# Layer 0 of a hybrid encoder projects x without its norm, and starts while x and weights land

## The chip, the core and the metric

The kernel runs on one core of a Trainium2 chip. Its engines are PE (matrix products), ACT (functions and copies, line by line), DVE and POOL (elementwise work), and SP, which only issues DMAs here. Each has its own queue and takes its instructions in order; they wait for one another by semaphores. PE reads operands from SBUF and writes sums to PSUM, from where ACT and DVE fetch them. The metric is device time in microseconds, the median over runs.

## The reference, cut to what matters

Two layers (`DEPTH = 2`) over 256 positions of width 2048:

```python
h = x
for i in range(DEPTH):
    hn = _rmsnorm(h, norm_g[i])                       # h * rsqrt(mean(h*h) + eps) * gain
    u = hn @ w_in[i]
    a_val, a_glu, a_z, q, k, v, b_z = jnp.split(u, offs, axis=-1)
    ya = _conformer_conv(a_val, a_glu, ...)           # GLU, depthwise conv of width 31, LayerNorm, SiLU
    ya = ya * jax.nn.silu(a_z)
    yb = _window_attention(q, k, v, bias_band, sink[i]) * jax.nn.silu(b_z)
    h = h + jnp.concatenate([ya, yb], axis=-1) @ w_out[i]
    e = _rmsnorm(p[i] @ w_pe[i], pe_g[i])             # embedding
    h = h + e * jax.nn.sigmoid(h @ w_pg[i])
return _rmsnorm(h, final_g)
```

The norm's root is one number per position. It can therefore be applied to x ahead of the projection, or to the projection's results, per position.

## The kernel before

All matrices stand transposed: 128 channels on the partitions, 256 positions along the free axis. A product of 128 x 128 weights with 128 x 256 of the input is made three times, since weights and input are each split into a high part in a shortened format and a low part, the rest (`mm3`, L398: high x high, high x low, low x high; L401 to L403).

Weights come as halves: 1024 columns of 128 partitions, 512 KB. Two make a chunk of 1 MB, loaded by SP into one of three raw buffers (`load`). `split` casts a half on ACT (L168) to its high part and subtracts it on DVE (L171) for the low part, into one of five buffers. The program asks for splits some four halves ahead (`ahead`, `get`); a half feeds 24 products on PE. Halves are numbered in the order of use in a layer: 0 to 3 embedding (`w_pe`), 4 to 11 the first two tiles of the convolution group's value and gate columns, 12 to 35 its other six tiles, 36 to 39 k, 40 to 43 v, then b_z and q by turns, then a_z, w_out, w_pg.

The order on PE, ACT and DVE is that of the program text (`manual_schedule`). After each half `pump` runs: it moves side generators on by one step (embedding's squares, the bias table, attention) and then takes some steps of the convolutions, 3.3 per half in this part of the layer. A step is a tap, one instruction on DVE (L566), but for the first of a tile, which is ACT's.

The start of layer 0: PE warms up with products of zeros; x, p and chunks of weights are loaded over the queues of SP and ACT. Embedding's products p @ w_pe run first, unsplit, straight from the raw weights (L487), while ACT squares x and DVE sums the squares (L392). From the sum come the root of the norm as a column (`rstd_col`: products with ones, a power on POOL, L361) and as a row over positions (`rstd_row`). `operand` then multiplies x by gain and row on DVE (L455) and splits it (L458, L459) into `hg`, the projection's input. A tile's result goes from PSUM through `glu`: ACT's sigmoid (L575), DVE's multiply (L576). k is split by ACT and DVE into `keys` (L599, L601); the gates zb pass Silu on ACT (L688); q is scaled and split into `qq` (L695 on ACT, L696 on DVE), which the scores `sc` (L636) need on PE. Embedding's squares are summed on POOL (L392), beside the convolution tiles; the bias table (`bias_prep`) has one product on PE (L329) and a copy on DVE (L331).

Of the kernel before, what the change touches and what calls it, by code (L numbers as in the profile page):

```python
# [10 lines left out]
F32 = mybir.dt.float32  # L11
# [45 lines left out]
NWARM = 6  # L57
QQ = ((4, 5), (2, 4))
# [21 lines left out]
def weight_halves():  # L80
# [39 lines left out]
HALVES = weight_halves()  # L120
NHALF = len(HALVES)
# [8 lines left out]
def trunk_kernel(ctx: ExitStack, tc: tile.TileContext, xT, pT, wst, par, gain, relb, sinkp, onehot, out):  # L130
# [23 lines left out]
    state = {"raw": -1, "spl": 3, "credit": 0.0}  # L154
# [8 lines left out]
    def split(h):  # L163
        raw = raws[h // 2][:, h % 2, :]
        w = wspl.tile([P, 2 * HALF + 64], F32R, tag="w", name=f"w{h}")
        w = w[:, SHIFT:SHIFT + 2 * HALF].rearrange("p (t n) -> p t n", t=2)
        hi, lo = w[:, 0], w[:, 1]
        nc.scalar.copy(hi, raw)  # L168
        spl[h] = w
        if h not in (4, 5):  # L170
            nc.vector.tensor_sub(lo, raw, hi.bitcast(F32))  # L171

    def first_lo(h):

        w = spl[h]
        nc.vector.tensor_sub(w[:, 1], raws[h // 2][:, h % 2, :], w[:, 0].bitcast(F32))

    def ahead(h):

        while state["spl"] < min(h, TOT - 1):  # L180
# [4 lines left out]
            if HALVES[n % NHALF][0] != "w_pe" or n >= NHALF:  # L185
                split(n)
            state["spl"] = n

    def get(h):

        r = h % NHALF
        if r < 12:
            ahead(h + (r | 1) + 2 - r)
        else:
            ahead(h + LS)
        return spl.pop(h)
# [66 lines left out]
    def load_p(l):  # L263
        pf = wk.tile([P, 2, S], F32, name=f"p{l}", tag="v", bufs=1)
        (nc.sync if l == 0 else nc.gpsimd).dma_start(pf, pT[l])
        return pf

    def load_half(c, x, eng=nc.sync, n=1):

        if c not in raws:  # L270
            raws[c] = wraw.tile([P, 2, HALF], F32, tag="raw", name=f"raw{c}")
        w = HALF // n
        for i in range(n):
            eng.dma_start(raws[c][:, x, i * w:(i + 1) * w], wst[c, :, x * HALF + i * w:x * HALF + (i + 1) * w])

    def load_x(k, eng=nc.sync):
        eng.dma_start(h[k // 8][:, k % 8:k % 8 + 4, :], xT[:, k:k + 4, :])

    h = halves(bigt("x"))

    load_half(0, 0, nc.scalar, 2)
    pf = load_p(0)
    load_half(0, 1)
    load_x(0, nc.scalar)
    load_x(4)
    load_half(1, 0, nc.scalar)
    load_x(8)
    load_x(12)
    load_half(1, 1)
    load_half(2, 0)  # L290
    gains = cst.tile([P, (DEPTH + 1) * KT], F32, name="gains")
    nc.sync.dma_start(gains, gain)
    load_half(2, 1)
    state["raw"] = 2
    pars = cst.tile([P, DEPTH * PW], F32, name="pars")
    nc.sync.dma_start(pars, par)
# [16 lines left out]
    nc.sync.dma_start(relt[0:NUM_BUCKETS, :], relb)  # L313
    oh = wk.tile([NUM_BUCKETS + 1, NREL], F32, name="oh", tag="sq", bufs=3)
    nc.sync.dma_start(oh, onehot)
    sinkt = cst.tile([P, DEPTH * NQ], F32, name="sinkt")
    nc.sync.dma_start(sinkt, sinkp.partition_broadcast(P))
# [94 lines left out]
    def steps(os, X, starts, stop):  # L412

        parts = []
        for _ in os:
            name, _, k0, nk = HALVES[Cursor.h % NHALF]
# [22 lines left out]
    for l in range(DEPTH):  # L439

        e = halves(bigt(f"e{l}"))
        eacc = wk.tile([P, 2, S], F32, name="eacc", tag="hacc")
# [26 lines left out]
        def copied(j, b, e=e):  # L469
            nc.scalar.copy(e[j // 8][:, j % 8:j % 8 + 2, :], b)  # L470

        for q in range(4):
            n = Cursor.h
            Cursor.h += 1
            if l:
                w = get(n).rearrange("p t (j k c) -> p t j k c", j=4, k=2)
            else:
                raw = raws[n // 2][:, n % 2, :].rearrange("p (j k c) -> p j k c", j=4, k=2)
            for jj in range(0, 4, 2):
                j = 4 * q + jj  # L480
                b = bank("e")
                for x in range(2):
                    for k in range(2):
                        if l:
                            mm3(b[:, x, :], w[:, :, jj + x, k, :], pp[:, :, k, :], x == 0 and k == 0, k == 1)
                        else:
                            nc.tensor.matmul(b[:, x, :], raw[:, jj + x, k, :], pf[:, k, :], start=x == 0 and k == 0,  # L487
                                             stop=k == 1, skip_group_check=True)
                if l == 0 and j // 2 < 4:
                    for k in (4 * (j // 2), 4 * (j // 2) + 2):  # L490
                        if k < KT - 2:
                            square_acc(hacc, h[k // 8][:, k % 8:k % 8 + 2, :], k == 0, nc.vector)
                    if j // 2 == 3:
                        sq = wk.tile([P, 2, S], F32, name="sq", tag="sq", bufs=3)
                        nc.scalar.activation(sq, h[1][:, 6:8, :], AF.Square)
                        hparts = halves_of(sq) + [fold(hacc)]
                if j // 2 == QQ[l][0]:
                    dg = rstd_col(hparts, D, f"rh{l}")
                    ahead(5 if l == 0 else Cursor.h - 1 - q + 5)
                if j // 2 == QQ[l][1]:  # L500
# [439 lines left out]
```

## Time and profile before

| | |
|---|---|
| median of 3 runs | 936.67 us (936.56 to 936.84) |
| the profiled execution's own time | 938.7 us |
| its span, first to last instruction | 936.9 us |
| mean granted clock of PE | 0.996 |
| PE busy | 923.9 us, 99% |
| DVE busy | 767.6 us, 82% |
| ACT busy | 549.2 us, 59% |
| POOL busy | 82.0 us, 9% |
| HBM read | 177.09 MB |

How to read it: the busy time of PE is modelled, and a PE that is busy is not PE at its peak. Rows of a timeline give start, duration, engine, line, operation, tiles and, in brackets, how long the engine stood idle before it and for whom. Rows of windows give, for each engine, busy time and number of instructions, then the granted clock, the share of busy DMA engines and GB/s. The chain is followed back from the last instruction, at each step to what released it.

### The profile page before, as it was taken

The page shows a single profiled execution, that of the slowest core. Times are in us where ns is not written, and L with a number is a line of the kernel's source. Part 1 is how long each engine was busy: PE and PEld are TensorE (multiplying, and loading weights), DVE is VectorE, ACT ScalarE, POOL GpSimd, SP SyncE. Part 2 cuts the span into 40 slices and gives each one's busy share as a digit, 9 for nine tenths or more (in the row PEclk, how much of TensorE's full clock was granted, in tenths as well). Part 3 has the DMA queues.
Part 4 walks back from the last instruction along what each step waited for, and adds up shares of the span by engine and source line. Part 5 has one row for each costly group of instructions (what it writes and reads, how often), then busy time and mean ns, then how long its engine had stood idle before and what let it go on. Part 6 is the DMA issues. An engine that isn't in the chain of part 4 may idle for free.

```text
span 936.9 us, 19106 instructions
## 1 busy us (share of the span) xinstructions
PE 923.9 (99%) x7960; PEld 909.7 (97%) x7960; DVE 767.6 (82%) x1282; ACT 549.2 (59%) x830; POOL 82.0 (9%) x79
## 2 busy tenths in 40 slices
PE   8999999999999999999999999999999999999995
PEld 7999999999999999999999999999999999999995
DVE  3999999998887786787679999999888877777663
ACT  4655454878874555554566445568788546445551
POOL 0013001001000000011102100100100000000111
PEclk9999999999999999999999999999999999999999
DMA  7674656555547455546555556565555554654532
GB/s 298 226 250 150 220 180 230 190 196 175 189 171 247 166 209 212 191 181 230 211 189 193 181 212 226 174 213 196 183 169 180 193 197 152 247 183 179 200 114 91
DMA packets 29011, 182.55 MB, mean 195 GB/s; under 512 B 3595, under 2 KB 4156, under 8 KB 9084
## 3 DMA queue, kind: packets, MB, share of 16 engines
q1 hardware_dynamic: 24284, 165.70, 50.1%
q0 software_dynamic: 3344, 12.88, 4.2%
q10 hardware_dynamic: 1296, 2.75, 0.8%
q8 instruction: 62, 1.02, 0.4%
q14 instruction: 25, 0.20, 0.1%
HBM read 177.09 MB, written 4.23 MB: 194 GB/s over the span
## 4 chain that ended last, share of the span: by engine, by line
PE 75%; DVE 19%; ACT 2%; issue 2%; DMA 1%; ACTq 0%; DVEq 0%
DVE cz L566 8%; DVE w L171 8%; PE o L401 6%; PE o L402 6%; PE o L403 6%; PE g L401 6%; PE g L403 6%; PE g L402 6%; PE ag L403 4%; PE ag L401 4%; PE ag L402 4%; PE za L401 3%; PE za L403 3%; PE za L402 3%; PE av L679 2%
## 5 line engine op out<-in xcount | busy, mean ns | idle before, releaser
L171 DVE TENSOR_TENSOR w<-raw,w 128x1024 fp32r<-128x1024 f32 x306 | 375.1, 1234 | 99.5 <-ACT w L168 98.6
L168 ACT CAST w<-raw 128x1024 fp32r<-128x1024 f32 x308 | 315.6, 1046 | 157.8 <-PE ag L403 42.5
L566 DVE SCALAR_TENSOR_TENSOR cz<-az,pars,cz 128x241 f32<-128x241 f32 (+11 forms) x480 | 215.9, 499 | 1.0
L401 PE MATMUL ag<-hg,w 128*128 128x256 f32 x512 | 141.8, 277 | 0.0
L403 PE MATMUL ag<-hg,w 128*128 128x256 f32 x512 | 141.6, 277 | 0.0
L402 PE MATMUL ag<-hg,w 128*128 128x256 f32 x512 | 141.5, 276 | 0.0
L403 PE MATMUL g<-h,w 128*128 128x256 f32 x512 | 141.3, 276 | 0.0
L401 PE MATMUL g<-h,w 128*128 128x256 f32 x512 | 141.3, 276 | 0.0
L402 PE MATMUL g<-h,w 128*128 128x256 f32 x512 | 141.3, 276 | 0.0
L401 PEld LDWEIGHTS ag<-hg,w 128*128 128x128 f32 x512 | 96.1, 188 | 0.9 <-ACT u L575 0.8
L403 PEld LDWEIGHTS ag<-hg,w 128*128 128x128 f32 x512 | 96.2, 188 | 0.1
L402 PEld LDWEIGHTS ag<-hg,w 128*128 128x128 f32 x512 | 96.1, 188 | 0.0
L401 PEld LDWEIGHTS g<-h,w 128*128 128x128 f32 x512 | 96.1, 188 | 0.0
L402 PEld LDWEIGHTS g<-h,w 128*128 128x128 f32 x512 | 96.1, 188 | 0.0
L403 PEld LDWEIGHTS g<-h,w 128*128 128x128 f32 x512 | 96.1, 188 | 0.0
L401 PE MATMUL za<-hg,w 128*128 128x256 f32 x256 | 71.7, 280 | 0.0
L401 PE MATMUL o<-yb,w 128*128 128x256 f32 x256 | 71.6, 280 | 0.0
L401 PE MATMUL q<-hg,w 128*128 128x256 f32 x256 | 71.5, 279 | 0.0
L401 PE MATMUL zb<-hg,w 128*128 128x256 f32 x256 | 71.5, 279 | 0.0
L402 PE MATMUL o<-yb,w 128*128 128x256 f32 x256 | 71.0, 277 | 0.0
L402 PE MATMUL q<-hg,w 128*128 128x256 f32 x256 | 71.0, 277 | 0.0
L403 PE MATMUL zb<-hg,w 128*128 128x256 f32 x256 | 71.0, 277 | 0.0
(223 smaller groups left out, 2264.4 us busy)
## 6 DMA issues: line engine op xcount, KB each, us to landing
raw<-in_wst SPq DMA_DIRECT2D x153, 1024.0 KB, 4.9
bias<-fscr POOLq DMA_DIRECT2D x16, 384.0 KB, 3.9
raw<-in_wst SPq DMA_DIRECT2D x4, 512.0 KB, 7.9
az<-in_xT POOLq DMA_DIRECT2D x4, 512.0 KB, 6.0
hscr<-e POOLq DMA_DIRECT2D x2, 1024.0 KB, 5.6
az<-hscr POOLq DMA_DIRECT2D x4, 512.0 KB, 5.4
x<-in_xT SPq DMA_DIRECT2D x3, 512.0 KB, 8.2
out_t<-og ACTq DMA_DIRECT2D x4, 256.0 KB, 3.0
```

What stands on the lines that cost most here:

```text
L168: nc.scalar.copy(hi, raw)
L171: nc.vector.tensor_sub(lo, raw, hi.bitcast(F32))
L401: nc.tensor.matmul(o, w[:, 0], x[:, 0], start=start, stop=False, skip_group_check=True)
L402: nc.tensor.matmul(o, w[:, 0], x[:, 1], start=False, stop=False, skip_group_check=True)
L403: nc.tensor.matmul(o, w[:, 1], x[:, 0], start=False, stop=stop, skip_group_check=True)
L566: nc.vector.scalar_tensor_tensor(acc[:, t, lo_:hi_], a[:, t, lo_ + s:hi_ + s], w(k), acc[:, t, lo_:hi_], ALU.mult, ALU.add)
L679: nc.tensor.matmul(o[hh * HD:(hh + 1) * HD, x, :], v[:, kt, g * HD:(g + 1) * HD], pt[hh][:, kt, :], start=x == 0 and kt == 0, stop=kt == 1 ...
```

## The change

In layer 0 the projection's input is x times gain, without the root. So it does not wait for the sum of squares: x and the weights of the first two tiles are loaded in pieces, in the order of use, and PE runs their products in four blocks of four k-tiles. ACT makes the high part of x times gain and DVE the low part (one instruction each per k-tile); weights are split by half a half (`split_part`). The sums of squares are made by POOL, and the root's column is asked for in the fourth block.

Every result of layer 0's projection is then multiplied by the root: in `evicted`, a DVE instruction that reads PSUM and writes a tile in SBUF (value and gate columns, k, b_z, q, a_z), and for v by the scale of ACT's copy. Sigmoid, Silu, the splits of k and the scaling of q read that tile.

Embedding's products of layer 0 come behind the first two tiles, split like all others (96 products instead of 64 plain ones), and the evictions of the two tiles stand between them. p, parameters and tables are loaded later, from `small_loads`; each of four tiles gets a memset on DVE ahead of it. `embed` (the bias table and embedding's squares) begins behind embedding's products. One warm-up product is added, the root of embedding's norm is asked for five steps later, and layer 1 keeps its order.

```diff
-NWARM = 6
+NWARM = 7
...
-    for q in range(4):
-        out.append(("w_pe", q, 0, 2))
+    if l:
+        out += W_PE
     for ts in FIRST_TILES:
...
+        if l == 0 and len(ts) == 2:
+            out += W_PE
...
+    def split_part(h, c):
+        if h not in spl:
+            w = wspl.tile([P, 2 * HALF + 64], F32R, tag="w", name=f"w{h}")
+            spl[h] = w[:, SHIFT:SHIFT + 2 * HALF].rearrange("p (t n) -> p t n", t=2)
+        raw = raws[h // 2][:, h % 2, c]
+        hi, lo = spl[h][:, 0, c], spl[h][:, 1, c]
         nc.scalar.copy(hi, raw)
+        nc.vector.tensor_sub(lo, raw, hi.bitcast(F32))
...
+    nc.sync.dma_start(gains, gain)
+    load_part(0, 0, nc.scalar)
+    load_x(0, 2)
+    load_part(1, 0, nc.scalar)
+    load_x(2, 2)
+    load_part(2, 0, nc.scalar)
+    load_part(3, 0)
     load_x(4)
+    for x in range(4):
+        load_part(x, 1)
     load_x(8)
+    load_part(4, 0)
+    load_part(5, 0)
     load_x(12)
+    load_part(6, 0)
+    load_part(7, 0)
+    for x in range(4, 8):
+        load_part(x, 1)
...
+    def small_loads():
+        for t in (pf[:, 0, 0:1], pars[:, 0:1], oh[:, 0:1], sinkt[:, 0:1]):
+            nc.vector.memset(t, 0.0)
+        nc.sync.dma_start(pf, pT[0])
+        nc.sync.dma_start(pars, par)
+        nc.sync.dma_start(relt[0:NUM_BUCKETS, :], relb)
+        nc.sync.dma_start(oh, onehot)
+        nc.sync.dma_start(sinkt, sinkp.partition_broadcast(P))
...
+            firsts = [bank(f"ag{l}_{t}") for t in range(2)]
+            for n in range(4):
+                c = slice((n % 2) * (HALF // 2), (n % 2 + 1) * (HALF // 2))
+                ks = range(4 * n, 4 * n + 4)
+                for y in range(4):
+                    for k in ks[2 * y:2 * y + 2]:
+                        i, kk = k // 8, k % 8
+                        hi, lo = (x[:, kk, :] for x in halves(hg[i]))
+                        nc.scalar.activation(hi, h[i][:, kk, :], AF.Copy, scale=gcol(l, k))
+                        nc.vector.scalar_tensor_tensor(lo, h[i][:, kk, :], gcol(l, k), hi.bitcast(F32),
+                                                       ALU.mult, ALU.subtract)
+                    split_part(4 * (n // 2) + y, c)
+                if n == 2:
+                    small_loads()
+                for k in ks[::2]:
+                    square_acc(hacc, h[k // 8][:, k % 8:k % 8 + 2, :], k == 0)
+                for y in range(4):
+                    if n == 3 and y == 2:
+                        dg = rstd_col(halves_of(hacc), D, f"rh{l}")
+                    w = spl[4 * (n // 2) + y].rearrange("p t (k c) -> p t k c", k=8)
+                    for k in ks:
+                        mm3(firsts[y // 2][:, y % 2, :], w[:, :, k % 8, :], hg[k // 8][:, :, k % 8, :],
+                            y % 2 == 0 and k == 0, k == KT - 1)
...
+            hilo(pp[:, 0], pp[:, 1], pf)
+            ahead(9)
+            rcol = dg
+            scaled = rstd_row(dg, f"rh{l}", settle=2)
+
+        def evicted(b, scale=None, scaled=scaled):
+            if scaled is None:
+                return b
+            u = wk.tile([P, 2, S], F32, name="ev", tag="sq", bufs=3)
+            if scale is None:
+                nc.vector.tensor_mul(u, b, bcast2(scaled))
             else:
+                nc.vector.scalar_tensor_tensor(u, b, scale, bcast2(scaled), ALU.mult, ALU.mult)
+            return u
...
         def glu(t, b):
+            b = evicted(b)
             u = wk.tile([P, S], F32, name=f"u{l}_{t}", tag="sg")
             nc.scalar.activation(u, b[:, 1, :], AF.Sigmoid)
             nc.vector.tensor_mul(a[:, t, :], b[:, 0, :], u)
             conv_q.append(conv(t))
...
+        if l == 0:
+            for q in range(4):
+                n = Cursor.h
+                Cursor.h += 1
+                w = get(n).rearrange("p t (j k c) -> p t j k c", j=4, k=2)
+                if q < 2:
+                    glu(q, firsts[q])
+                for jj in range(0, 4, 2):
+                    copied(4 * q + jj, epair(w, jj, pp))
+                pump()
...
-            yield from wait(10)
+            yield from wait(15)
...
-        b = pair(hg, f"k{l}")
+        b = evicted(pair(hg, f"k{l}"))
...
-            b = pair(hg, f"zb{l}_{i}")
+            b = evicted(pair(hg, f"zb{l}_{i}"))
             nc.scalar.activation(zb[:, i:i + 2, :], b, AF.Silu)
             b = pair(hg, f"q{l}_{i}")
+            qs = -(HD ** -0.5)
+            if l == 0:
+                b, qs = evicted(b, qs), 1.0
...
-            b = pair(hg, f"za{l}_{t}")
+            b = evicted(pair(hg, f"za{l}_{t}"))
```

More of the change, by code (lines that the diff above doesn't have):

```diff
@@ L56 @@
 AW = (0,0,0,0)
[L57 to L58 removed]
+NWARM = 7
+QQ = (2, 4)
 FIRST_TILES = [(0, 1)] + [(t,) for t in range(2, NCT)]
@@ L117, in weight_halves @@
     return out
-HALVES = weight_halves()
-NHALF = len(HALVES)
+W_PE = [("w_pe", q, 0, 2) for q in range(4)]
+HALVES = [weight_halves(l) for l in range(DEPTH)]
+NHALF = len(HALVES[0])
+HALVES = sum(HALVES, [])
 NCHUNK = NHALF // 2
@@ L163, in split @@
     def split(h):
[L164 to L176, printed above, removed]
+        split_part(h, slice(0, HALF))
+    def split_part(h, c):
[4 more added lines that the diff above has]
+        hi, lo = spl[h][:, 0, c], spl[h][:, 1, c]
+        nc.scalar.copy(hi, raw)
+        nc.vector.tensor_sub(lo, raw, hi.bitcast(F32))
     def ahead(h):
@@ L439, in trunk_kernel @@
     for l in range(DEPTH):
-        e = halves(bigt(f"e{l}"))
-        eacc = wk.tile([P, 2, S], F32, name="eacc", tag="hacc")
+        if l:
+            e = halves(bigt(f"e{l}"))
+            eacc = wk.tile([P, 2, S], F32, name="eacc", tag="hacc")
         hg = []
@@ L467, in trunk_kernel, with copied @@
         ecopy = []
-        def copied(j, b, e=e):
+        def copied(j, b):
             nc.scalar.copy(e[j // 8][:, j % 8:j % 8 + 2, :], b)
[L472 to L475, printed above, removed]
-                w = get(n).rearrange("p t (j k c) -> p t j k c", j=4, k=2)
-            else:
[L478 to L500, printed above, removed]
-                    rbs.append(rstd_row(dg, f"rh{l}", copy=False))
-                    if l == 0:
-                        first_lo(4)
-                        operands(0, 1)
-                        first_lo(5)
-                        subs.pop(0)()
-                        operands(2, 1)
-                if QQ[l][1] + (l == 0) <= j // 2 <= QQ[l][1] + 1:
-                    operands(4 * (j // 2 - QQ[l][1]), 2)
-                ecopy.append((j, b))
-                while ecopy and 4 * (l == 0) <= j // 2 < 6:
-                    copied(*ecopy.pop(0))
-            pump()
@@ L577, in glu, with embed @@
             conv_q.append(conv(t))
-        for ts in FIRST_TILES:
+        if l == 0:
+            e = halves(bigt(f"e{l}"))
+            eacc = wk.tile([P, 2, S], F32, name="eacc", tag="hacc")
+            for q in range(4):
+                n = Cursor.h
+                Cursor.h += 1
+                w = get(n).rearrange("p t (j k c) -> p t j k c", j=4, k=2)
+                if q < 2:
+                    glu(q, firsts[q])
+                for jj in range(0, 4, 2):
+                    copied(4 * q + jj, epair(w, jj, pp))
+                pump()
+        def embed(l=l, eacc=eacc, e=e):
+            if l == 0:
+                yield from wait(4)
+                bias_prep()
+                yield from wait(4)
+            for j in range(0, KT, 2):
+                yield from wait(2)
+                square_acc(eacc, e[j // 8][:, j % 8:j % 8 + 2, :], j == 0)
+            yield from wait(12 + 8 * l)
+            es = fold(eacc)
+            yield from wait(3)
+            dg = rstd_col([es], D, f"re{l}")
+            yield from wait(15)
+            eb = rstd_row(dg, f"re{l}", "reb")
+            yield from wait(50)
+            while not state["enorm"]:
+                yield
+            for j in range(KT):
+                d = e[j // 8][:, j % 8, :]
+                nc.vector.scalar_tensor_tensor(d, d, pcol(l, PO_PE + j), eb, ALU.mult, ALU.mult)
+                yield
+        state["enorm"] = False
+        engen = embed()
+        side.append(engen)
+        for ts in FIRST_TILES[l == 0:]:
             bs = [bank(f"ag{l}_{t}") for t in ts]
```

116 lines of the change are left out of this document (55 added, 61 removed).

## The prediction, made before the changed kernel was run

> **What bounds the kernel now.** I read the page first: busy times, and the chain that ended last.
>
> ```profile
> PE 923.9 (99%) x7960; PEld 909.7 (97%) x7960; DVE 767.6 (82%) x1282; ACT 549.2 (59%) x830; POOL 82.0 (9%) x79
> PE 75%; DVE 19%; ACT 2%; issue 2%; DMA 1%; ACTq 0%; DVEq 0%
> ```
>
> PE looks like the only bound, yet a fifth of the chain runs over DVE. The chain in order of time, asked for two windows, shows where (start, duration, what):
>
> ```profile
> 48.58 0.13 PE ag L403
> ...
> 49.01 1.05 ACT w L168
> 50.08 1.02 DVE w L171
> ...
> 162.00 0.70 DVE qq L696
> ...
> 174.68 0.60 ACT az L688
> 175.28 0.95 ACT w L168
> 176.25 1.23 DVE w L171
> ...
> 188.66 0.70 DVE qq L696
> 189.41 0.97 PE sc L636 x6
> ```
>
> From 49 to 189 us, layer 0 hangs on DVE: splitting weights (L171), convolution taps (L566), then the operand qq of the second head group, for which the scores on PE wait. After 189.41 the chain is PE's. The table of windows (PE, PEld, DVE, ACT, POOL, clock) confirms it:
>
> ```profile
> 53.58:164.04 110.46, 110.28 (x973) 110.07 (x972) 109.43 (x184) 54.95 (x71) 16.58 (x12) 1.00 0.57 201
> 164.04:189.40 25.36, 25.27 (x216) 25.06 (x216) 23.91 (x54) 20.73 (x40) 1.44 (x2) 1.00 0.58 199
> 5.00:10.00 5.00, 4.54 (x21) 3.46 (x20) 0.00 (x0) 0.00 (x0) 0.00 (x0) 1.00 1.03 419
> 15.00:20.00 5.00, 3.85 (x20) 3.20 (x20) 3.05 (x5) 4.23 (x7) 1.63 (x1) 0.82 1.06 383
> 20.00:25.00 5.00, 5.00 (x23) 4.26 (x22) 3.52 (x7) 2.14 (x5) 0.00 (x0) 0.84 0.29 75
> ```
>
> In the first stretch DVE idles 1.0 us of 110. So two engines are full at once, and whatever DVE must do more before 189 us moves the end by its whole length; what PE saves at the start counts only if DVE too comes earlier to this stretch.
>
> **The change, part by part.** PE's start, from the timeline of PE and DVE:
>
> ```profile
> 24.69 0.47 PE L401 MATMUL ag<-hg,w 128*128 128x256 f32 x1
> 42.01 1.03 PE L329 MATMUL fps<-oh,relt 33*16 33x511 f32 x2
> 48.53 0.28 PE L401 MATMUL ag<-hg,w 128*128 128x256 f32 x1
> 50.08 3.50 DVE L171 TENSOR_TENSOR w<-raw,w 128x1024 fp32r<-128x1024 f32 x3 [0.51 <-ACT w L168]
> 24.01 1.65 DVE L455 SCALAR_TENSOR_TENSOR hn<-x,gains,rh0b 128x256 f32<-128x256 f32 x4
> 66.60 2.29 DVE L566 SCALAR_TENSOR_TENSOR cz<-az,pars,cz 128x248 f32<-128x248 f32 x3
> 66.78 1.44 POOL L392 TENSOR_TENSOR eacc<-eacc,sq 128x512 f32<-128x512 f32 x1 [3.88 <-ACT sq L391]
> 69.94 1.25 DVE L566 SCALAR_TENSOR_TENSOR cz<-az,pars,cz 128x255 f32<-128x255 f32 x3
> ```
>
> Before, 192 products of the first two tiles run from 24.69 to 48.53, with the bias table's product (1.03) among them; the first split of the third tile's later halves (half 16 of layer 0) leaves DVE at 53.58. Prices: three splits take 3.50, so neighbours overlap by 0.08 and one costs 1.14; half of one 0.60; a 128x256 operand 0.39; one POOL add of 128x512 beside DVE lengthens three taps from 1.25 to 2.29, so DVE loses 1.04.
>
> Evictions and ACT's part, by form and from the timelines:
>
> ```profile
> L683 DVE TENSOR_TENSOR az<-av,az 128x512 f32<-128x512 f32 x8 | 5.5, 684 | 0.0
> L818 ACT ACTIVATE og<-e,gains 128x256 f32<-128x256 f32 x16 | 7.2, 493 | 0.0
> 11.10 1.13 ACT L391 ACTIVATE sq<-x 128x512 f32<-128x512 f32 x2
> 42.12 0.38 ACT L575 ACTIVATE u<-ag 128x256 f32<-128x256 f32 x1
> 42.40 1.99 ACT L168 CAST w<-raw 128x1024 fp32r<-128x1024 f32 x2
> 579.30 1.50 ACT L599 CAST keys0h<-k 64x256 fp32r<-64x256 f32 x4 [1.67 <-PE k L403]
> 580.82 1.50 ACT L599 CAST keys1h<-k 64x256 fp32r<-64x256 f32 x4
> 582.35 1.73 DVE L601 TENSOR_TENSOR keys0l<-k,keys0h 64x256 fp32r<-64x256 f32 x4 [0.47 <-ACT keys1h L599]
> 163.35 0.69 DVE L696 SCALAR_TENSOR_TENSOR qq<-q,qq 64x512 fp32r<-64x512 f32 x1 [0.66 <-ACT qq L695]
> 43.07 0.68 DVE L331 COPY fs<-fps 16x511 f32<-16x511 f32 x1 [0.82 <-PE fps L329]
> raw<-in_wst ACTq DMA_DIRECT2D x2, 256.0 KB, 5.8
> raw<-in_wst SPq DMA_DIRECT2D x153, 1024.0 KB, 4.9
> 18.13 1.63 POOL L361 TENSOR_TENSOR rh0col<-rh0v,mhalf 128x2 f32<-128x2 f32 x1 [16.81 <-DVE rh0v L359]
> ```
>
> *Start, PE and ACT.* x and the eight first halves are 6 MB; at 383 to 419 GB/s the last lands near 20, so arrival does not bind for long. A first piece of 256 KB lands near 5.5: issued at 0.7, it took a median of 5.8 for two pieces of which one queued behind the other, and I take 4.8 for the one ahead. With a scaled copy and a split behind it, products start near 7.0. Each of four blocks (four slices of x, four half-pieces of weights) needs on PE 48 products, at 110.46 us for 973 about 0.1135 each: 5.4, and 2.72 for the 24 of a half; on ACT four scaled copies of 0.40 (0.493 less overlap), four casts of 0.53 (half of 1.05) and two squares of 0.54: 4.8.
>
> *Start, DVE.* Four low parts of x at 0.39 and four half splits at 0.60: 4.0 a block. But the squares' sums, which DVE made, now go to POOL, one for the first block and two for each later one, and take 1.04 each from DVE: 6.1 against PE's 5.4. The first block is paced by arrival and ends on DVE near 10.3; ACT's squares hold the second to 11.9, and from there DVE is full: 18.0, 24.4 (with four memsets of 0.08), 30.5. PE follows each half split: 13.0, 19.4, 26.9, and with the root's column products (0.9) 34.3. POOL's power (1.63) hides behind the last two halves.
>
> *Start, queues.* There are three raw buffers for four chunks, so pieces 6 and 7 wait on SP until DVE has split pieces 0 and 1 (14.7), and all loads behind them wait too; they land near 17.5, when ACT comes to them. The small loads wait for DVE's memsets at 24.4, and SP holds the next chunk behind them: it lands near 31.4 (4.9 after its issue at 26.5), in time for PE. If it came 3 us later it would cost PE directly.
>
> *Embedding.* The root's row reaches ACT at 35.4, and only behind that copy does ACT cast halves 10 to 12, so DVE, done with half 9 at 34.8, idles 1.6. Before, 64 plain products ran in PE's wait; now 96 split ones run from 35.0 to 45.9. Meanwhile the first two tiles' evictions, sigmoids, the copies of embedding's banks, the convolutions' first steps and the splits alternate on ACT and DVE; counted through in order, half 16 leaves DVE at 54.6, 1.0 later than before. Without any idle DVE would need, from 6.0 on, 6.2 for low parts, 9.6 half splits, 7.3 lost to POOL, 10.2 for nine splits, 4.3 for eleven taps and 3.0 for the rest: 40.6, so 46.6, 7.0 earlier. I take +1.0, since the waits named stand in a fixed order, and keep -7 to +3. The seventh warm-up product lies in PE's wait: 0.
>
> On that lock, the Trainium skill (SBUF — State Buffer, section SBUF: two separate sides) says that a POOL instruction holds the shared port pair to its end and DVE, with two SBUF inputs, fully blocks. The 1.04 beside an add of 1.44 agrees in kind; by that rule seven adds would take 10.1 instead of 7.3, and the total would be 2.8 more, 961.6; the sum goes by the row.
>
> *Tiles 2 to 7.* Each product now goes through DVE (PSUM times row, 0.684, so 0.60) before its sigmoid. DVE's order is eviction, multiply; the multiply waits for ACT's sigmoid (0.38 and two handovers of 0.03, 0.44), which before had run far ahead. ACT's next cast also stands behind that sigmoid, so DVE, done with the multiply (0.33), waits 0.62 for it. 0.60 + 0.44 + 0.62 = 1.66, six times: 10.0. The waits lie between 0, if other ACT work were ahead, and 1.06; the row of L575 with the cast right behind it is the order in question, so I take all.
>
> *k.* Eviction 0.60; then ACT's eight casts, 579.30 to 582.32, after which alone DVE starts in the layer-1 row: 3.1. In all 3.7 (0.60 at least).
>
> *bias table.* Its DVE copy and negation (0.7) move behind half 16: 0.7; PE's 1.03 moves too and is hidden, since PE waits for DVE.
>
> *zb and q.* The first gate: eviction 0.60, then Silu (0.60) and cast (1.05) before DVE's next split: 2.2. The second: 2.0, on the chain's own ACT steps at 174.68. Each q: eviction 0.60 and one ACT scaling (0.6, the wait of 0.66 at 163.35) that now stands behind it: 1.25, twice 2.5. v is scaled by ACT in the copy that it had, 0. The later gates and q run beside DVE with room (the chain is PE's there): 0, at most 3.25 for one group more. Conv pulls begin two halves earlier, but the count per half stays, so they relieve nothing before 189.
>
> Sum: 1.0 + 10.0 + 3.7 + 0.7 + 2.2 + 2.0 + 2.5 = 22.1. The profiled execution took 938.7 around a span of 936.9; runs have a median of 936.67, so the span stands for them: 936.7 + 22.1 = 958.8.
>
> **The rivals.**
> *Faster: PE leads after all.* If DVE did not bind, PE would begin the third tile at 45.9, or, unheld from 7.0, at 41.3 (21.8 + 0.9 + 0.7 + 10.9), and still have the bias product to do: 48.53 - 41.3 - 1.0 = 6.2 gained, 930.5; with 45.9, 935.1. It decides if DVE's qq comes before PE asks for it. Against it: even with no idle at all DVE's work gives -7.0 + 11 evictions x 0.60 + 0.7 = +0.3. It needs the POOL adds to cost DVE next to nothing.
> *Same:* that +0.3, 937.0, every wait hidden.
> *Evictions alone:* ACT's order costs nothing; +1.0 + 6.6 + 0.7 = 8.3, 945.0. For it: ACT is half idle (54.95 of 110.46). Against: the idle is behind, not ahead of, what it waits for.
> *Worse:* PE now stands for some 6 us at the first scores, and the clock windows above show that a thin stretch at 15 to 18 us is followed by half clock, 0.82 and 0.84 over two windows of 5, 1.7 us of work. With that on PE's path and two more head groups delayed, 22.1 + 1.7 + 2x3.25 = 30.3: 967.0. The Trainium skill (TensorE: Matmul & The Clock Gate, Part 1) says the same in general, that after an idle window of about 3.4 us the clock is halved; the rows agree.
>
> **How the numbers follow.** Forecast 0.55, evictions alone 0.18, worse 0.12, faster 0.10, same 0.05. The likeliest by itself: start -7 to +3, k's wait away (-3.1) or one group more (+3.25), so 948 to 964. The range takes in evictions alone and stops short of the whole of worse: 942 to 964; beyond lie faster, same and most of worse. About 0.2% (1.9 us) is what a measurement tells from no change: slower 0.85, same 0.05, faster 0.10.
>
> **What would show it.** Right: in the profile after, the chain still runs over DVE to about 210 us; waits of DVE for ACT's sigmoid some 0.4 each at six tiles, for ACT's cast right behind, 3 us once before the keys' low parts; PE idle of several us ahead of k's neighbours and the scores; PE at the third tile near 46; half 16 off DVE near 55; DVE taps of 1.5 beside POOL's sums at the start. Wrong: qq ready at or before 164, PE without gaps from 8 us on; or sums on POOL that cost DVE nothing; or gaps on DVE that are absent because ACT's order differs.

## The result, and the profile after

The changed kernel takes 964.38 us (median of 6 runs, 962.94 to 967.28), the one before 936.62 in the runs beside it: ratio 1.0298, interval 1.028 to 1.0315. It is slower by 27.8 us, where 22.1 were forecast. The profiled execution took 962.94 around a span of 961.1, 24.2 more than the span of before; what follows accounts for these 24.2. The other 3.5 are the choice of executions: the profiled one was 2.1 above its median before and 1.4 below it after. One execution of x10 (1560.33 us) and one of x12 (3320.83 us) were in a slower state and are left out below.

The page of the changed kernel: busy times, and the chain that ended last by engine.

```profile
PE 933.8 (97%) x7994; PEld 918.8 (96%) x7994; DVE 783.7 (82%) x1305; ACT 554.1 (58%) x852; POOL 91.7 (10%) x86
PE 80%; DVE 14%; ACT 3%; issue 1%; DMA 1%; SPq 0%; ACTq 0%; DVEq 0%
```

PE fell from 99 to 97%: it now stands still at times. The chain runs over DVE until later than before, but with pieces of ACT and PE between, so that DVE's share of it is smaller and ACT's larger. The windows of the stretch that DVE filled before (PE, PEld, DVE, ACT, POOL, clock, DMA share, GB/s), and the last rows of the chain in order of time ahead of the second head group's scores:

```profile
54.48:149.70 95.22, 86.25 (x712) 82.96 (x711) 88.04 (x146) 39.22 (x56) 15.35 (x11) 0.99 0.49 170
149.70:208.40 58.70, 55.04 (x451) 54.26 (x449) 53.42 (x106) 33.40 (x53) 4.60 (x6) 0.96 0.57 197
...
205.64 0.61 DVE ev L562
206.28 0.64 ACT qq L761
206.94 0.68 DVE qq L762
207.65 0.70 DVE qq L762
208.40 0.98 PE sc L699 x6
```

DVE, which before idled 1.0 us of 110, now idles 7.2 of 95, and PE 9.0. The second scores start at 208.40 instead of 189.41: 19.0 us. Two more terms follow. Half for half, PE's shift against before grows from 19.0 to 20.3 in the rest of layer 0 and stays there to its end. In layer 1 it grows by 5.0 to 25.4, of which 0.7 come back later on: net 4.3. (In x12, which has the order of before, PE gains the same 0.7 on the profiled execution of before, so that belongs to this execution.) The last 0.5 come back at the end.

What goes on at one eviction, from the timelines of DVE and of ACT (start, duration, idle time before it in brackets):

```profile
75.32 0.67 DVE L560 TENSOR_TENSOR ev<-ag,rh0rb 128x512 f32<-128x512 f32 x1
76.47 0.42 DVE L594 TENSOR_TENSOR az<-ev,u 128x256 f32<-128x256 f32 x1 [0.48 <-ACT u L593]
77.41 1.23 DVE L178 TENSOR_TENSOR w<-raw,w 128x1024 fp32r<-128x1024 f32 x1 [0.52 <-ACT w L177]
...
76.02 0.42 ACT L593 ACTIVATE u<-ev 128x256 f32<-128x256 f32 x1 [8.24 <-DVE ev L560]
76.35 2.93 ACT L177 CAST w<-raw 128x1024 fp32r<-128x1024 f32 x3
```

ACT had been idle for 8.24 us, standing in its order at the sigmoid, which needs DVE's eviction. DVE then waits 0.48 for that sigmoid and 0.52 for the cast behind it. All engines have time; it is lost in handing over. The waits of the changed kernel between 50 and 210 us (engine and line, waited for: total, times, longest) show all six tiles:

```profile
ACT u L593 <- DVE ev L560: 47.8, 6, 8.6
DVE w L178 <- ACT w L177: 7.2, 11, 1.6
DVE az L594 <- ACT u L593: 2.9, 6, 0.5
PE sc L699 <- DVE qq L762: 3.7, 4, 2.8
```

Layer 1, windows of 100 us each of the kernel before and of the changed one (the same work, shifted by 20):

```profile
495.00:595.00 100.00, 100.00 (x885) 100.00 (x884) 97.82 (x161) 51.74 (x68) 12.49 (x8) 1.00 0.55 194
...
515.00:615.00 100.00, 100.00 (x852) 100.00 (x851) 93.98 (x154) 49.84 (x66) 13.29 (x8) 1.00 0.52 186
```

PE is busy without a gap and at the full granted clock in both, and yet does 852 products instead of 885. The starts of neighbouring products lie 117.8 ns apart instead of 113.3, from 501.7 to 643.5 us. The forecast knew nothing of that.

### The profile page after: what moved, and what is told of

Its sections match the earlier page's. It is cut to its first block, busy times and chain, and to the rows that moved or that the text cites. A ratio compares the mean times of both kernels' runs of the same rounds, so it can differ in the third digit from the quotient of the medians.

```text
span 961.1 us, 19270 instructions
## 1 busy us (share of the span) xinstructions
PE 933.8 (97%) x7994; PEld 918.8 (96%) x7994; DVE 783.7 (82%) x1305; ACT 554.1 (58%) x852; POOL 91.7 (10%) x86
## 4 chain that ended last, share of the span: by engine, by line
PE 80%; DVE 14%; ACT 3%; issue 1%; DMA 1%; SPq 0%; ACTq 0%; DVEq 0%
PE o L416 6%; PE o L415 6%; PE g L417 6%; PE o L417 6%; PE g L415 6%; PE g L416 6%; DVE cz L583 6%; DVE w L178 5%; PE ag L417 4%; PE ag L415 4%; PE ag L416 4%; PE za L415 3%; PE za L417 3%; PE za L416 3%; PE q L415 2%; PE q L416 2%
## 5 line engine op out<-in xcount | busy, mean ns | idle before, releaser
L178 DVE TENSOR_TENSOR w<-raw,w 128x1024 fp32r<-128x1024 f32 (+1 forms) x320 | 384.7, 1212 | 112.6 <-ACT w L177 111.9
L177 ACT CAST w<-raw 128x1024 fp32r<-128x1024 f32 (+1 forms) x320 | 319.0, 1023 | 124.4 <-PE g L417 28.1
L583 DVE SCALAR_TENSOR_TENSOR cz<-az,pars,cz 128x241 f32<-128x241 f32 (+13 forms) x480 | 215.7, 500 | 1.9 <-ACT cz L576 1.0
L417 PE MATMUL ag<-hg,w 128*128 128x256 f32 x512 | 143.8, 281 | 3.4 <-DVE w L178 3.4
L415 PE MATMUL ag<-hg,w 128*128 128x256 f32 x512 | 143.2, 280 | 2.7 <-ACT w L177 2.7
L416 PE MATMUL ag<-hg,w 128*128 128x256 f32 x512 | 142.9, 279 | 0.0
L415 PE MATMUL zb<-hg,w 128*128 128x256 f32 x256 | 73.5, 287 | 2.6 <-ACT w L177 2.6
L417 PE MATMUL zb<-hg,w 128*128 128x256 f32 x256 | 72.9, 285 | 0.8 <-DVE w L178 0.8
L416 PE MATMUL zb<-hg,w 128*128 128x256 f32 x256 | 72.7, 284 | 0.0
L415 PE MATMUL q<-hg,w 128*128 128x256 f32 x256 | 71.7, 280 | 0.0
```

What stands on the lines that cost most here:

```text
L415: nc.tensor.matmul(o, w[:, 0], x[:, 0], start=start, stop=False, skip_group_check=True)
L416: nc.tensor.matmul(o, w[:, 0], x[:, 1], start=False, stop=False, skip_group_check=True)
L417: nc.tensor.matmul(o, w[:, 1], x[:, 0], start=False, stop=stop, skip_group_check=True)
L583: nc.vector.scalar_tensor_tensor(acc[:, t, lo_:hi_], a[:, t, lo_ + s:hi_ + s], w(k), acc[:, t, lo_:hi_], ALU.mult, ALU.add)
```

## The experiments

The gauge in most of them is the place of the second head group's scores on PE, since the time behind it has causes of its own: of their eight products the third, which the chain shows in both kernels (before 189.41, changed 208.40). "Half n" counts weight halves as in the prediction. The start scatters from run to run: with the same code, half 16 leaves DVE 0.2 to 2.9 us later than before, and the scores follow. The stretch from there to the scores hardly scatters: 135.83 us before and in x12, 153.92 in the changed kernel, and 153.93 to 153.95 in x6, x7, x8, x14 and x15, which leave its code alone. So 18.1 us are lost in it, and of a place of the scores about 2 us are open.

**Without evictions (x1_no_evict).**

```
 def evicted(b, scale=None, scaled=scaled):
-    if scaled is None:
-        return b
+    return b
```

> The changed kernel without its evictions in layer 0: the results of layer 0 are not multiplied by the root, and sigmoid, Silu and the casts read the banks as before; the new start is kept. Theory 1 (the time is lost because every eviction lies on DVE's full stretch and DVE and ACT then wait for each other): the second head group's scores fall back from 208.4 to 187-190 us, DVE's waits for the sigmoid vanish, 933-938 us, up to 5 more if layer 1's matmuls keep the slower pace (117.8 ns instead of 113.3) that they show in the changed kernel. Theory 2 (the loss is the new start: POOL's sums beside DVE and splits that wait for ACT): the scores stay beyond 200 us and the time beyond 950.

Measured: 943.29, ratio 1.0064 (1.0047 to 1.0081), just above what theory 1 allows with the slower pace. From PE's timeline:

```profile
189.85 0.34 PE L698 MATMUL sc<-keys0h,qq 128*128 128x256 f32 x1
```

The scores are back (the stretch takes 136.09), so the loss belongs to the evictions and their order, and theory 2 falls. But the new start by itself gains nothing: PE begins the third tile 1.5 us earlier than before, and DVE, full behind it, is at the scores as late as ever. Another 4.3 us stand in layer 1, with 117.8 ns a product from 482.0 us on, as in the changed kernel.

**The evictions without the new start (x3_before_evict).** In the kernel before:

```
+scaled = wk.tile([P, S], F32, name="onerow", tag="rb", bufs=1)
+nc.vector.memset(scaled, 1.0)
 ...
-b = pair(hg, f"k{l}")
+b = evicted(pair(hg, f"k{l}"))      # likewise glu, zb, q, za
```

> The kernel before, with its own start, plus the same evictions in layer 0 (a multiplication by a row of ones, so nothing of the result changes). Theory 1: all of the loss but the start's 0.9 and the bias table's 0.7, with the first two tiles' evictions and waits added (up to 3.3): second scores at 207-210 us instead of 189.4, 954-958 us, and 113.3 ns a matmul in layer 1 or 4 us more if the slower pace comes with any shift of the work. Theory 2 (start): scores near 190-197, 937-945 us.

Measured: 959.77, ratio 1.0243 (1.0227 to 1.0258). Scores from PE's timeline:

```profile
210.07 0.39 PE L653 MATMUL sc<-keys0h,qq 128*128 128x256 f32 x1 [0.21 <-DVE qq L716]
```

The loss up to the scores (20.7, with the first two tiles' evictions in it) comes with the evictions alone; the stretch behind half 16 takes 153.82 us, in the changed kernel 153.92. Layer 1 stays at 113.3 ns here: evictions and a shift of the work do not bring the slower pace, something in the new start does. The time is 1.8 above what was expected, since another 2.2 us came in the rest of layer 0, which the expectation had at nothing.

**Whose time is it: the evictions' or the waits'? (x2_act_reads_banks, x5_act_first).** x2 lets ACT read the bank instead of the evicted tile; x5 issues ACT's reading ahead of the eviction as well:

```
-b = evicted(b)
+pb, b = b, evicted(b)                     # x2
+nc.scalar.activation(u, pb[:, 1, :], AF.Sigmoid)
 ...
+nc.scalar.activation(u, b[:, 1, :], AF.Sigmoid)   # x5: sigmoid first,
+b = evicted(b)                                    # then the eviction
```

> The changed kernel with every eviction kept on DVE, but ACT's sigmoids, Silus and casts of layer 0 read the bank, not the evicted tile, so that they need not wait for DVE (the root is thereby left out of their operands). Theory 1: the evictions' own time stays (6 tiles, k, 2 gates, 2 q, each 0.60: 6.6, with start and bias table 8.3) and the waits go: second scores near 198 us, 945 us, up to 5 more with layer 1's slower pace. Rival (the evictions' length and what PE and the banks do with it is all, ACT's order costs nothing): scores stay near 208, 960-964 us.

> As x2_act_reads_banks, but in layer 0 ACT's sigmoids, Silus and casts are also issued ahead of the eviction of their bank, since in x2 they still waited for it, as the second reader of one bank (the root is left out of their operands). Theory 1 (evictions 0.6 each, and the same again in DVE's waits for ACT): waits of DVE for sigmoid and next cast go, second scores near 198 us instead of 208.4, 949-951 us with layer 1's slower pace as in the changed kernel. Rival (the evictions' length and PE's waits for DVE are all; ACT's order costs nothing): scores stay at 206-209, 961-963 us.

x2: 962.48, ratio 1.0268 (1.0253 to 1.0284), scores at 208.9; it settled nothing. The row of its waits shows why (the same row as in the changed kernel): two engines that read one bank are put in order, and the sigmoid stood behind the eviction again.

```profile
ACT u L593 <- DVE ev L560: 47.8, 6, 8.6
```

The Trainium skill (PSUM — Partial Sum Buffer, "PSUM bank collisions raise a hardware error") says that two engines that touch one bank (in the same 32 partitions) must be ordered, reads against reads too. The row agrees that they are.

x5 took that order away: 951.94, ratio 1.0157 (1.0142 to 1.0172). An eviction in DVE's timeline, and the scores from the chain:

```profile
85.29 0.68 DVE L560 TENSOR_TENSOR ev<-ag,rh0rb 128x512 f32<-128x512 f32 x1
86.00 0.42 DVE L594 TENSOR_TENSOR az<-ev,u 128x256 f32<-128x256 f32 x1
86.35 1.22 DVE L178 TENSOR_TENSOR w<-raw,w 128x1024 fp32r<-128x1024 f32 x1
...
195.18 0.94 PE sc L700 x6
```

No idle time stands before the multiply or the split; from 54 to 212 us DVE waits 0.2 us in all. The scores are 5.8 late instead of 19.0. The stretch behind half 16 takes 141.37 us: of the 18.1 lost, the evictions' own length is 5.5, the order of the two engines 12.6. The rival (length alone) falls. Layer 1 keeps the slower pace.

**A version that keeps the computation (x9_later).** What ACT and DVE make from an evicted tile is issued one weight half later:

```
-u = ...; sigmoid; multiply; conv_q.append(conv(t))
+later(gated)       # the same four lines, run at the next half's pump
 ...                # likewise Silu, q's scaling; the keys in two groups of four
```

> The changed kernel, all of its computation kept, with what ACT and DVE make from an evicted tile in layer 0 issued one weight half later (sigmoid and multiply of tiles 2 to 7, the keys' casts in two groups of four, Silu, q's scaling), so that a split stands between the eviction and what waits for it. Theory 1: as in x5_act_first only the evictions' own length stays, second scores at 194-198 us, 950-954 us with layer 1's slower pace. Rival (x5 gained because ACT ran far ahead, which a half's delay does not give): 957-962.

Measured: 956.82, ratio 1.0208 (1.0193 to 1.0224). Scores from PE's timeline, and one row of PE's waits:

```profile
196.68 0.28 PE L723 MATMUL sc<-keys0h,qq 128*128 128x256 f32 x1
...
PE pt L750 <- ACT s L744: 4.7, 1, 4.7
```

Up to the scores the expectation holds (7.3 late); the time is 2.8 above the expected end. The last q, put off like the others, makes the last attention late, and PE waits for it until 287.7; behind that wait the granted clock is 0.50 up to 293.9, and the shift has grown by 8.9 at half 93. A step that was put off on one engine was on time for DVE and late for PE.

**POOL's sums (x4_sums_on_dve, x11_sums_later).**

```
-square_acc(hacc, ..., k == 0)
+square_acc(hacc, ..., k == 0, nc.vector)    # x4: the start's sums on DVE
 ...
-yield from wait(4)
+yield from wait(48)                         # x11: embedding's sums later
```

> The changed kernel with the seven sums of squares of its start on DVE instead of POOL. By the price of 1.04 us that a POOL add costs DVE against some 0.6 for DVE's own add, DVE gains about 3 us in the start; half 16 leaves it at 52-54 instead of 54.5, and the time falls by 0 to 2.5: 961-964 us. If POOL's adds cost DVE nothing, the start becomes 4 longer and the time 966-968.

> The changed kernel with embedding's seven sums of squares on POOL moved behind layer 0's second scores. They stand in DVE's full stretch and by the row of before each costs DVE 1.04 us: second scores 7.3 earlier, at 201 us, and 955-957 us. If POOL beside DVE costs nothing, 961-964 us. If DVE pays later what it saves here, scores early and 961-964 all the same.

x4: 962.01, ratio 1.0264 (1.0249 to 1.028). As expected in size, but not settled by one run: PE's shift is 1.3 us lower than in the changed kernel from the third tile on to the end. The six profiles with these sums on DVE (x4, x10, x13, x16 to x18) have the third tile 1.7 to 4.0 us ahead of before, 2.7 in the mean; the ten that leave them on POOL and keep the start's seven warm-up products have it 0.5 to 2.6 ahead, 1.6 in the mean. x11: 960.33, ratio 1.0248 (1.0231 to 1.0265); scores from PE's timeline:

```profile
200.93 0.39 PE L699 MATMUL sc<-keys0h,qq 128*128 128x256 f32 x1 [0.21 <-DVE qq L762]
```

Moving seven sums by POOL brings the scores 7.5 forward; the stretch behind half 16 falls to 146.20, by 7.7 or 1.10 each (7.3 by the row of before, 1.04 each). But the sums now run from 229 to 274 us, beside the steps of attention on DVE, and by half 93 only 3.8 of the 7.5 are left: the third of the expected ways, in part. The time is 3.3 above the range expected of the first.

**Layer 1's pace (x6_addresses, x7_one_product, x8_warm8, x12_before_addresses, x14_small, x15_large).** The new order of the start makes the tiles of the program land at other SBUF addresses, in layer 1 too. x6 puts those of layer 1 where they were, by a one-column memset that touches `e` ahead of `hg`, and unused small tiles ahead of `pp`; x14 does that for the small tiles alone, x15 for the large alone, x12 moves the large tiles of the kernel before to the changed kernel's addresses. x7 and x8:

```
 operands(8 + 4 * t, 2); subs.pop(0)()
+if t == 0:
+    idle(1)                 # x7: one 128x128 product in layer 1
 ...
-NWARM = 7
+NWARM = 8                   # x8
```

> The changed kernel with the SBUF addresses of layer 1's operands as they are in the kernel before (large tiles and the buffers of pp and qq; two one-column memsets on POOL are added for it). Theory A (layer 1's pace of 117.8 ns from 489 to 641 us comes from the addresses of the operands): 113.3 ns there, 4.3 us less, 957-959 us. Theory B (a state of TensorE's pipeline that one of its own disturbances sets): no change, 962-964 us, or some other stretch at the slower pace.

> The changed kernel with one more product of 128x128 on TensorE in layer 1, about 5 us behind the place where its slower pace begins (502 us). Theory B (a state that the next disturbance can end): 113.3 ns behind it, 3.5 to 4.3 us less, 958-960 us. Theory A (addresses): the product costs its 0.3 us and the pace stays, 963-964 us.

> The changed kernel with one more warm-up product ahead of everything, in time in which TensorE waits for data. Addresses and layer 1's order stay; only the place of every later instruction in TensorE's stream moves by one. If the pace depends on that place, it changes in layer 1 (957-960 us); by theories A and B it does not: 962-965 us.

> The kernel before, with only the addresses of its large tiles moved to those of the changed kernel (by three one-column memsets on POOL); the order of the work is kept. By the addresses: layer 1's matmuls go to 117.8 ns from its first gate products until the next product of another kind on TensorE, some 50 halves x 0.11 us, up to 5.3 us slower, 938-942 us. If not the addresses: 936.5-937.5 us.

> The changed kernel with only the addresses of the small tiles (pp and qq among them) as in the kernel before; the large tiles stay where the change put them. Theory A1 (layer 1's slower pace is set where TensorE goes over to pp, and again from pp to hg, by pp's address): 113.3 ns in layer 1, 958-960 us. Theory A2 (by the large tiles' addresses, or by the two together): the pace stays 117.8 ns or changes in part, 962-965 us.

> The counterpart of x14_small: only the large tiles at their addresses of before, pp and qq where the change put them. Theory A1: 117.8 ns in layer 1 as in the changed kernel, 962-965 us. Theory A2: 113.3 ns, 958-960 us.

x6: 959.03, ratio 1.0233 (1.0216 to 1.025), 113.3 ns throughout layer 1's first stretch. x7: 959.92, ratio 1.0243 (1.0228 to 1.0258). x8: 965.84, ratio 1.0303 (1.0287 to 1.032), 117.8 ns as in the changed kernel. x12: 936.42, ratio 0.9993 (0.9983 to 1.0003), 113.3 ns. x14: 959.46, ratio 1.0244 (1.0228 to 1.0261). x15: 963.72, ratio 1.029 (1.0274 to 1.0306). The windows of 100 us in layer 1 of x14 and x15:

```profile
515.00:615.00 100.00, 100.00 (x884) 100.00 (x884) 97.49 (x161) 52.43 (x70) 12.42 (x8) 1.00 0.55 197
...
515.00:615.00 100.00, 100.00 (x851) 100.00 (x850) 93.97 (x153) 49.83 (x66) 13.31 (x8) 1.00 0.52 187
```

884 products with the small tiles at their old addresses, 851 with only the large ones back. So the small tiles decide, and theory A1 stands as far as that; which of them was not told apart (pp is the one that TensorE reads right ahead of the change of pace). And the pace is a state: x7's timeline of PE around its one added product, where neighbours start 0.12 apart before it and, after it, mostly 0.11 (3 products in 0.34 instead of 0.35); its windows of 100 us behind have 885.

```profile
508.66 0.28 PE L415 MATMUL ag<-hg,w 128*128 128x256 f32 x1
508.78 0.28 PE L416 MATMUL ag<-hg,w 128*128 128x256 f32 x1
508.90 0.28 PE L417 MATMUL ag<-hg,w 128*128 128x256 f32 x1
509.02 0.38 PE L361 MATMUL idle<-ident,ones 128*128 128x128 f32 x2
...
509.36 0.28 PE L416 MATMUL ag<-hg,w 128*128 128x256 f32 x1
509.48 0.28 PE L417 MATMUL ag<-hg,w 128*128 128x256 f32 x1
509.59 0.28 PE L415 MATMUL ag<-hg,w 128*128 128x256 f32 x1
509.70 0.28 PE L416 MATMUL ag<-hg,w 128*128 128x256 f32 x1
...
515.00:615.00 100.00, 100.00 (x885) 100.00 (x884) 97.05 (x160) 52.71 (x70) 12.47 (x8) 1.00 0.53 192
```

Both theories hold a part. In layer 1 addresses decide whether TensorE falls into the slower pace where it goes over to pp and again to hg, and in x7 one product of another kind ended it. But other products do not always do so: in the changed kernel four products for a norm (L368) at 614.81 leave the pace at 117.8. Nor is the slower pace new: the kernel before starts 87 products between 31.5 and 41.5 us and 90 between 53 and 63. What sets and ends the state stays open.

**All together (x10_all, x13_both, x16_behind_norm, x17_wait_for_sums, x18_fold_earlier).** x10 joins x9, x11, x4 and x6. Each of the next takes away the one stall that the trace of the last shows (the shorter waits around the sums, changed with it, are left out here):

```
-if l == 0:              later(heads)
+if l == 0 and i < 4:    later(heads)      # x13: last q groups not put off
-yield from wait(48)
+yield from wait(74)                       # x13: embedding's sums behind attention
+yield from wait(92)                       # x16: behind the normalization
+yield from wait(87)                       # x17: five halves earlier, the fold five halves further behind
-yield from wait(1)
+yield from wait(4)                        # x18: fold four halves ahead of its product
```

> All together, all of the computation kept: the changed start and evictions, x9's later steps, x11's later sums, x4's sums on DVE and x6's addresses. By the prices measured so far: second scores at 208.4 - 13 (waits) - 7 (POOL's sums) - 1.3 = 187 us, or where PE's own work sets them (-2 to -4 against the kernel before), 113.3 ns in layer 1: 933-937 us. If moved sums and later steps fill what they free: 940-945 us.

> As x10_all, with the two repairs that its trace asks for: only the first two q groups are put off, so that the last attention is not late for the end of the first half of layer 0 (5.0 us of waiting on TensorE, and a shift of 13 us between the halves 76 and 93 with what follows it), and embedding's sums go behind the attention, one each weight half. By x10's shift of -3.8 us at half 64 and no loss behind it: 932-936 us. If the sums or the convolutions' rest hold TensorE there again: 940-946 us.

> As x13_both, with embedding's sums on POOL put still later, behind the convolution's normalization: in x13 they lengthened DVE's subtractions for it by 1.1 us each, and POOL's power for its root stood behind one of them, after which TensorE waited 2.61 us at 316.4. If that was the 5.7 us that x13 lost between the halves 93 and 110, what is left is x13's shift at half 76 to 93, -0.7 to 0: 934.5-937 us. If it was the convolutions' rest or the attention, 941-943 us as in x13.

> As x16_behind_norm, whose trace kept a shift of -0.7 us against the kernel before up to half 110 and then had TensorE wait 2.79 us for the fold of embedding's sums, with half clock behind it, 5.1 in all; here five weight halves stand between the last sum and its product instead of none, and the sums begin five halves earlier. If that wait was all: 5.1 less than x16's profiled run, some 937 us for it (no change against before); if the sums again collide with the normalization, as in x13: 941-943 us.

> As x17_wait_for_sums, with the fold of embedding's sums issued four weight halves ahead of its product instead of one: in x17 DVE came to it behind a split that itself waited for TensorE, so that TensorE waited 4.62 us at 362.9 in its turn, and the shift went from +0.2 at half 110 to +8.6. If that is all, the shift stays at -0.7 to +0.5 and the profiled run takes 936-939 us, no change against before; if the sums beside the splits are the cost, 943-948.

x10: 949.07, ratio 1.0121 (1.0101 to 1.014). x13: 943.26, ratio 1.0065 (1.0052 to 1.0077). x16: 945.4, ratio 1.0091 (1.0076 to 1.0105). x17: 948.54, ratio 1.0127 (1.0106 to 1.0148). x18: 938.1, ratio 1.0014 (1.0005 to 1.0023). x10 and x17 lie above both of their expected ranges, and so does the median of x16. In the order x10 (scores, then its stall), x13, x16, x17, from timelines and waits:

```profile
188.70 0.28 PE L730 MATMUL sc<-keys0h,qq 128*128 128x256 f32 x1
283.43 0.69 PE L757 MATMUL pt<-ident,s 128*128 128x128 f32 x2 [4.72 <-ACT s L751]
...
PE rv0b L382 <- POOL rv0col L375: 2.3, 1, 2.3
...
359.64 0.58 PE L368 MATMUL re0c<-ones,fold 128*128 128x1 f32 x4 [2.51 <-DVE fold L393]
...
362.93 0.99 PE L368 MATMUL re0c<-ones,fold 128*128 128x1 f32 x4 [4.34 <-DVE fold L393]
```

In x10 the scores come 0.7 earlier than before, and then the last attention is late (4.72). In x13 that is gone, and POOL's power for the convolution's root stands behind a moved sum (2.3). In x16 and x17 PE waits for the fold, which stands on DVE behind weight splits: in x16 splits that the sums beside them have lengthened (2.32 instead of 1.22), in x17 splits that the chain reaches over ACT's casts from PE's own products. x17's expectation missed that, since it moved the sums and left the fold next to its product. In x18 PE waits as follows, ahead of the first product (first row) and from 12 to 900 us (the others, 1.5 in all):

```profile
PE ag L415 <- ACT w L177: 2.5, 1, 2.5
...
PE pt L757 <- ACT s L751: 0.8, 2, 0.4
PE o L417 <- DVE w L178: 0.4, 1, 0.4
PE o L416 <- DVE yb L862: 0.3, 1, 0.3
```

Some 26 of the changed kernel's 27.8 us are gone with all of its computation kept: they were order, addresses and, in a small part, the engine that sums the squares. But x18 does not beat the kernel before; it is 0.14% above it, at the edge of what can be told. Its third tile comes 1.7 us ahead of before, but 1.2 of that is the bias table's product, which only moved behind it; and between the halves 110 and 130, where embedding's sums now stand, PE loses 1.4. How the rest divides was not told apart.

## Why the prediction missed, and what of it held

- **The step that failed: all that stands behind the second scores was put at nothing.** The sum ends at the scores ("whatever DVE must do more before 189 us moves the end by its whole length") and takes PE's work behind them, layer 1 with it, as long as before; no term and no rival names layer 1. Layer 1's instructions are the same, but their products went at 117.8 ns instead of 113.3, which cost 5.0 us in the profile (net 4.3). Without the slower pace the same kernel takes 959.03 (x6), 959.92 (x7) and 959.46 (x14), inside the range; with it, it passes the range's end at 964.
- **That these three come so near to 958.8 is luck in part.** At the scores the sum was 3.1 too high (k, gates and q, less 1.05 missing behind tile 7). Another 1.3 us came in the rest of layer 0, which "the later gates and q run beside DVE with room: 0" had left out. And 3.5 more came from holding one profiled execution for the median, as the result says.
- **Direction and cause up to the scores: right.** Slower, because DVE's stretch up to the second scores grows. The marks named for it are there, all but k's wait of 3 us: the chain over DVE and ACT up to 208.4, the sigmoid's wait (0.48 against 0.44), the cast's behind it (0.51 against 0.62), six times. x1, x3 and x5 show that it is the cause and not only beside it.
- **Start: right in the trace, with luck.** Half 16 leaves DVE at 54.48 (54.6 forecast), PE begins the third tile at 46.06 (45.9). But in other runs of this start half 16 leaves DVE 0.2 to 2.9 late, where 1.0 was forecast. The first product came at 8.87 instead of 7.0: x's first piece was there at 6.11 instead of 5.5, and only then did ACT load a table for 1.28 us, which before it had done at 2.71, while it waited for data; the forecast had no term for it. At the third tile nothing of this is left.
- **Tiles 2 to 7: right.** DVE's low parts are 0.90 late at half 16 and 11.49 at half 40; less the bias table's 0.7 that is 9.9, against 10.0. Another 1.05 come by half 43, where the last of embedding's sums on POOL stands, which before lay inside the stretch.
- **k: too dear.** 3.7 forecast, 1.65 measured (half 43 to 44). The step "eight casts, after which alone DVE starts" failed: in layer 0 DVE begins the keys' low parts behind the first casts and waits 0.47 and 0.41, and in layer 1 of the same kernel it does wait for the eighth cast, 2.39, from DVE's timeline.

```profile
142.14 0.85 DVE L661 TENSOR_TENSOR keys0l<-ev,keys0h 64x256 fp32r<-64x256 f32 x2 [0.47 <-ACT keys0h L659]
143.41 0.86 DVE L661 TENSOR_TENSOR keys0l<-ev,keys0h 64x256 fp32r<-64x256 f32 x2 [0.41 <-ACT keys0h L659]
...
606.75 1.73 DVE L661 TENSOR_TENSOR keys0l<-k,keys0h 64x256 fp32r<-64x256 f32 x4 [2.39 <-ACT keys1h L659]
```

The difference between the rows is the operand: k in its PSUM bank, which ACT and DVE both read (x2 shows two readers of a bank put in order), against the evicted tile in SBUF. The forecast took a row of the first kind for work of the second. No run tests this by itself.

- **zb and q: somewhat too dear.** The gates cost 1.9 and 2.0 (2.2 and 2.0 forecast), the first q 1.0 and the second next to nothing in DVE's order (1.25 each). With k that makes 19.0 instead of 22.1 at the scores.
- **Clock gate: right in size, not certain to come.** The rival "worse" charged 1.7 us for one stretch at half clock. The windows of the changed kernel around its two long waits of PE, each 3.41 us ahead of half clock and at it:

```profile
144.56:147.97 3.41, 1.03 (x6) 0.83 (x7) 3.21 (x7) 3.38 (x6) 0.00 (x0) 1.00 0.00 0
147.97:151.39 3.42, 3.42 (x18) 3.42 (x17) 3.42 (x8) 2.66 (x5) 0.00 (x0) 0.50 0.17 31
178.70:182.11 3.41, 1.63 (x11) 1.46 (x12) 2.37 (x4) 3.23 (x5) 0.00 (x0) 1.00 0.59 247
182.11:185.52 3.41, 3.41 (x18) 3.41 (x17) 3.41 (x8) 0.97 (x2) 0.00 (x0) 0.50 0.02 5
```

Half of 3.41 us is 1.7. Both stretches fall where DVE is busy throughout (3.42 and 3.41), so they cost nothing that DVE had not cost. In x9, where PE's wait was on the path, the stretch behind it was. The Trainium skill (TensorE: Matmul & The Clock Gate, Part 1) puts half clock behind an idle window of some 3.4 us. The length agrees; but here PE was busy for 1.03 and 1.63 us of that window, so no wholly idle one was needed.

- **POOL's lock: both agree in kind, and the row gave the size.** Beside a sum on POOL one tap on DVE takes 1.51 instead of 0.47, by 1.04 longer, and x11 gives 1.10 a sum. The Trainium skill (SBUF — State Buffer, section SBUF: two separate sides) has DVE blocked for the whole length of a POOL instruction that began first. A sum with nothing of DVE beside it took 1.30 (x17, at 343.84), so DVE loses most of that; the 1.44 by which the prediction reckoned the rule was measured with DVE at work beside it.

## What to carry to other kernels

Where two engines are both full or nearly so, a new step between them costs its own length and, as long as its consumer is issued right behind it, the handing over there and back: here 5.5 and 12.6 us. Issue something else between the new step and what needs it, then look at what this makes late next, for nearly every step put off here turned up as another engine's wait further on. And when the part of a kernel that was not edited changes its pace, count the instructions in equal windows and compare the addresses before looking for a cause in the edit.

## What the hardware showed that was not expected

- Products of 128x128 by 128x256 follow one another at 113.3 or at 117.8 ns, with the clock granted in full and no wait shown. Both are steady for dozens of halves (885 and 852 in 100 us). In layer 1 the slower one begins where TensorE goes over to another operand. It came in all runs of the new start with its own addresses of the small tiles (851 or 852 where counted above), except that one added product ended it in x7. It came in none with the addresses of the kernel before (884 or 885). An estimate from the Trainium skill (TensorE: Matmul & The Clock Gate, Part 1), 256 columns at 2.4 GHz and a fixed 2.5 ns, is 109.2; neither pace is that.
- DVE and POOL lengthen each other: embedding's seven sums, alike in size, took 1.3 to 2.2 us each in x17, by what DVE did beside them, and DVE's splits beside them 1.7 to 2.3 instead of 1.22.
- One and the same start differs from run to run, and half clock is a part of it. The kernel before had half clock from 18.18 to 21.59 us in its profiled execution. x12, with the same order, had none there, though PE was busy for 2.26 of the 3.41 us ahead of it in both, and it began the third tile 1.44 earlier. The windows of the kernel before and of x12:

```profile
18.18:21.59 3.41, 3.41 (x10) 2.67 (x10) 1.11 (x2) 3.25 (x6) 1.57 (x1) 0.50 0.68 263
...
18.18:21.59 3.41, 3.29 (x17) 2.59 (x16) 2.32 (x4) 3.41 (x7) 1.58 (x1) 1.00 0.77 285
```
